# Side steps of one stage left to the products of the next, in a decoder block on one NeuronCore

## The chip, the cores and the metric

The kernel runs on one core of one Trainium2 chip. The metric is the device time of one execution in microseconds (us). Beside it stands one execution taken by the hardware profiler, whose span goes from the first to the last instruction of the program. The engines are PE (TensorE, matrix products), DVE (VectorE), ACT (ScalarE), POOL (GpSimd) and SP (which issues most DMA transfers). PSUM is the memory into which PE writes its sums; the kernel uses it as two pools of four tiles of 128 x 512 floats.

## The reference

One decoder layer on 256 tokens with 2048 features, all in f32:

```python
proj = rmsnorm(h, g_mix) @ w_in              # q, k, v, z, xBC, dt, two gates
out_a = attention(q, k, v) @ w_attn_br       # sliding window, with sinks
out_s = rmsnorm(ssd(...) * silu(z), g_ssd) @ w_ssd_br
merged = sigmoid(g_a) * out_a + sigmoid(g_s) * out_s
h = h + merged @ w_o
f = rmsnorm(h, g_ffn)
h = h + (silu(f @ w_gate) * (f @ w_up)) @ w_down
gate = sigmoid(rmsnorm(h, g_ple) @ w_ple_gate)
h = h + gate * (p @ w_ple_proj)
out = rmsnorm(h, g_final)
```

## The kernel before

**Products.** Every f32 product is made of three: a number is split into a high part (fp32r) and the low rest, and hi x hi, hi x lo and lo x hi are summed. Activations lie transposed, features on partitions, in tiles of four k-blocks of 128 features (`uT`, `yT`, `mergedT`, `hT`, `actT`, `h2T`); weights come in pieces of 128 x 1024 (`wr`, loaded by SP, four buffers), are split by ACT (`wh`, four buffers) and DVE (`wl`, three buffers), and are used by twelve matmuls of 512 columns.

**Wide blocks.** From the gate projection on, the work is a row of `wide_block` calls (L280): 256 tokens x 1024 columns, which give four sums `c11, c12, c21, c22`. The loop runs over pairs of k-blocks, `kp` = 0 to 7 (0 to 5 in the last third of `w_down`). A plain pair takes two weight pieces and 24 matmuls. One or two pairs of each block, named by the argument `forms`, are done with fewer matmuls, 21, in the manner of Strassen and Winograd: they need four combined "token forms" of the activations (`token_forms`, L267) and four combined weights (`tr`, four DVE additions, then split into `th` and `tl`). These form pairs sum into four further PSUM tiles, `shared`; after the block's last form pair their contents are combined into `mid` (one ACT, four DVE instructions), and when the block is done, `settle` or `add_settled` (L358, L363) joins each of the four sums with its part of `mid` on DVE.

**Pools.** The first line of `wide_block` is `psum.reverse()`: the four sums of a block come from the pool that held the `shared` tiles of the block before, and its `shared` tiles and all `aux_tile()` calls come from the pool that held the settled sums of the block before.

**Side steps.** Small pieces of work are queued in `side` and taken out by `pump`, one after each twelve matmuls, or two after a form pair (L97). A step of `queue_flip` (L980) or of `hidden` (L1041) is one `transpose_pair` (L144): four PE transposes of 128 x 128 into an `aux_tile()`, the split on ACT and DVE, and for a form pair `token_forms`. `square_sum` (L1020) is a step of ACT work for a norm; `rsqrt_mean` is one small DVE and one POOL instruction that give its factors (`r2`, `r3`, `r4`). `drain()` runs all steps that are left at once; it stands outside the blocks, so that their `aux_tile()` calls come before the next `psum.reverse()`.

**Order of the stages.** Gate projection `GSO` (2 blocks, forms `UPAIRS`), `w_ssd_br` (2 blocks, forms `YPAIRS`), `w_o` (2 blocks, forms at `mforms`), then three thirds of the feed-forward part: 4, 4 and 3 calls of `hidden` (one block each, forms at `hforms`, pairs 2 and 5), and after each third two blocks of `w_down` (forms at `aforms`), then projections with `nblock`, a plain loop with the same pieces and pumps, for `w_ple_proj` and `w_ple_gate`. The steps that a stage's last block queues are drained at L1011 (`merged` to `mergedT`), L1036 (`h` to `hT`, two `square_sum`), after the `hidden` calls of each third (`act` to `actT`) and at L1081 (`h` to `h2T`, two `square_sum`): six places. Between two blocks of one stage, `hidden` to `hidden` or the first block of `w_o` to the second, the steps are pumped within the next block.

The order in which each engine gets its instructions is drawn up when the program is built, by a planner that goes by priority (the order in the text) and by what it expects to be ready; what it finds not ready it lets others pass.

Of the kernel before, what the change touches and what calls it, by code (L numbers as in the profile page):

```python
# [23 lines left out]
NB = 512  # L24
# [6 lines left out]
FFN = 5632  # L31
# [30 lines left out]
def block_kernel(ctx: ExitStack, tc: tile.TileContext, x, x_t, p_t, positions, vecs, rows, g_final,  # L62
# [14 lines left out]
    def big(shape, dtype=F32, name="big"):  # L77
        return big_p.tile(shape, dtype, name=name, tag="big")

    def roll(name="roll"):  # L80
        return roll_p.tile([P, NB], F32, name=name, tag="roll")
# [13 lines left out]
    side, heads = deque(), deque()  # L95
# [7 lines left out]
    def drain(*queues):  # L103
        for q in queues or (side,):
            while q:
                q.popleft()()
# [22 lines left out]
    def split_to(dst, j0, ps, gains=None):  # L129

        if gains is None:
            nc.scalar.copy(out=dst[:, 0, j0:j0 + 2, :], in_=ps)
            nc.vector.tensor_tensor(out=dst[:, 1, j0:j0 + 2, :], in0=ps,
                                    in1=dst[:, 0, j0:j0 + 2, :].bitcast(F32), op=ALU.subtract)
        else:
            for j in range(2):
                nc.scalar.activation(out=dst[:, 0, j0 + j, :], in_=ps[:, j, :], func=AF.Copy,
                                     scale=gains[j])
                nc.vector.scalar_tensor_tensor(out=dst[:, 1, j0 + j, :], in0=ps[:, j, :],  # L139
                                               scalar=gains[j],  # L140
                                               in1=dst[:, 0, j0 + j, :].bitcast(F32),
                                               op0=ALU.mult, op1=ALU.subtract)
# [16 lines left out]
    def stat(tiles, k):  # L159
        return tiles[k // 4][:, 0, k % 4, :], tiles[k // 4][:, 1, k % 4, :]  # L160

    def mean_parts(n, eps, name):

        m = const.tile([P, NT, n + 1], F32, name=name)
        nc.vector.memset(m[:, :, n:n + 1], eps)
        return m
# [4 lines left out]
    def rsqrt_mean(parts, out_r):  # L171

        n = out_r.shape[1]
        s = stat_p.tile([P, NT], F32, name="rms_s")[:, :n]
        nc.vector.tensor_reduce(out=s, in_=parts, op=ALU.add, axis=AX.X)
        nc.gpsimd.tensor_tensor(out=out_r, in0=s, in1=mhalf[:, :n], op=ALU.pow)
# [82 lines left out]
    def joined(tiles, kp):  # L259

        ks = slice(2 * (kp % 2), 2 * (kp % 2) + 2)
        sc = roll("fsc").rearrange("p (j t) -> p j t", j=2)
        src = tiles[kp // 2].bitcast(F32)
        nc.vector.tensor_tensor(out=sc, in0=src[:, 0, ks], in1=src[:, 1, ks], op=ALU.add)
        return sc

    def token_forms(sc, dst):  # L267


        fm = roll("fm").rearrange("p (f t) -> p f t", f=4)  # L270
        a11, a21, a12, a22 = sc[:, 0, :P], sc[:, 0, P:], sc[:, 1, :P], sc[:, 1, P:]
        for o, x, y, op in ((fm[:, 0], a22, a21, ALU.subtract), (fm[:, 1], fm[:, 0], a11, ALU.add),
                            (fm[:, 2], a12, fm[:, 1], ALU.subtract),
                            (fm[:, 3], a11, a21, ALU.subtract)):
            nc.vector.tensor_tensor(out=o, in0=x, in1=y, op=op)
        nc.scalar.copy(out=dst[:, :, 0], in_=fm)
        nc.vector.tensor_tensor(out=dst[:, :, 1], in0=fm, in1=dst[:, :, 0].bitcast(F32),
                                op=ALU.subtract)
# [89 lines left out]
    def form_tiles(pairs, name):  # L368
        tile = big([P, 2, 4, 2, P], F32R, name=name)
        return {kp: tile[:, i] for i, kp in enumerate(pairs)}  # L370

    def column_pair(w, col0, jj):
        return tuple((w, col0 + (2 * jj + q) * NB) for q in range(2))
# [275 lines left out]
    ssq2 = mean_parts(GROUPS, SSM_EPS, "ssq2")  # L649
    GW = HPG * HD  # L650

    YPAIRS, yforms = (4,), {}

    def hslice(g):
        return slice(g * HPG, (g + 1) * HPG)
# [299 lines left out]
            nc.scalar.activation(out=merged[t][:, cols(j)], in_=accs[0][t], func=AF.Sigmoid,  # L955
                                 scale=r1[:, t:t + 1])
    drain(heads)
    UPAIRS = (2, 5)
    uforms = {}

    def u_forms(kp):
        def run():
            if kp == UPAIRS[0]:
                uforms.update(form_tiles(UPAIRS, "uforms"))
            token_forms(joined(uT, kp), uforms[kp])
        return run

    side.extend(u_forms(kp) for kp in UPAIRS)
    r2 = const.tile([P, NT], F32, name="r2")
# [10 lines left out]
    def queue_flip(src, dst, j, gbase=None, forms={}):  # L980
        for i in range(2):
            def run(i=i):
                if i == 0:
                    dst.extend(feat_tiles(1, "flipT"))
                gains = None
                if gbase is not None:
                    gains = [vcol(gbase, 4 * j + 2 * i + jj) for jj in range(2)]
                transpose_pair(src, j * NB + i * 2 * P, dst[j], 2 * i, gains, forms.get(2 * j + i))
            side.append(run)

    gates = []
    for jj in range(2):
# [3 lines left out]
            nc.scalar.activation(out=parts[i], in_=parts[i], func=AF.Sigmoid,  # L996
                                 scale=r1[:, i // 2:i // 2 + 1])
        gates.append(parts)
    mforms = form_tiles((4,), "mforms")
    for jj in range(2):  # L1000
        sums, parts = wide_block(column_pair(w_ssd_br, 0, jj), lambda k: stat(yT, k), KD, yforms)
        for i in range(4):
# [5 lines left out]
                                    op=ALU.add)  # L1008
        for q in range(2):
            queue_flip(merged, mergedT, 2 * jj + q, None, mforms)  # L1010
    drain()  # L1011


    h = [big([P, D], F32, name="h") for _ in range(NT)]
# [5 lines left out]
    def square_sum(j, ssq):  # L1020
        for t in range(NT):
            junk = roll("junk")
            nc.scalar.activation(out=junk, in_=h[t][:, cols(j)], func=AF.Square, scale=D ** -0.5,
                                 accum_out=ssq[:, t, j:j + 1])

    def add_to_h(jj, sums, parts):
        for i in range(4):
            add_settled(i, h[i // 2][:, cols(2 * jj + i % 2)], sums, parts)

    ssq3 = mean_parts(4, EPS, "ssq3")  # L1030
    for jj in range(2):
        add_to_h(jj, *wide_block(column_pair(w_o, 0, jj), lambda k: stat(mergedT, k), KD, mforms))
        for q in range(2):
            queue_flip(h, hT, 2 * jj + q, V_GFFN, hforms)
            side.append(lambda j=2 * jj + q: square_sum(j, ssq3))
    drain()  # L1036
    r3 = const.tile([P, NT], F32, name="r3")
    rsqrt_mean(ssq3, r3)


    def hidden(j, dst, kp0, forms):  # L1041
        sums, parts = wide_block(((w_gate, j * NB), (w_up, j * NB)), lambda k: stat(hT, k), KD,
                                 hforms)
        act = [roll("act") for _ in range(NT)]
        for i in range(4):
            settle(i, sums, parts, None if i % 2 else act[i // 2])
        for t in range(NT):
            nc.scalar.activation(out=act[t], in_=act[t], func=AF.Silu, scale=r3[:, t:t + 1])
            nc.vector.scalar_tensor_tensor(out=act[t], in0=parts[2 * t + 1],
                                           scalar=r3[:, t:t + 1], in1=act[t], op0=ALU.mult,  # L1050
                                           op1=ALU.mult)
        for i in range(2):
            side.append(lambda i=i: transpose_pair(act, i * 2 * P, dst, 2 * i, None,
                                                   forms.get(kp0 + i)))

    ssq4 = mean_parts(4, EPS, "ssq4")
    h2T, pT, gfin = [], None, None
    thirds = ((0, 4, (2, 5)), (4, 8, (2, 5)), (8, FFN // NB, (3,)))
    for j0, j1, apairs in thirds:
        last = j1 == FFN // NB  # L1060
        actT = []
        aforms = form_tiles(apairs, "aforms")
        for j in range(j0, j1):
            actT.append(big([P, 2, 4, SEQ], F32R, name="actT"))
            hidden(j, actT[-1], 2 * (j - j0), aforms)
        drain()
        if last:
            pT = [big([P, 2, 2, SEQ], F32R, name="pT")]
            pt = roll("pt").rearrange("p (j t) -> p j t", j=2)
            nc.gpsimd.dma_start(out=pt, in_=p_t)  # L1070
            split_to(pT[0], 0, pt)
            gfin = big([P, D], F32, name="gfin")
            nc.gpsimd.dma_start(out=gfin, in_=g_final.partition_broadcast(P))
        for jj in range(2):
            add_to_h(jj, *wide_block(column_pair(w_down[j0 * NB:j1 * NB], 0, jj),
                                     lambda k, a=actT: stat(a, k), 4 * (j1 - j0), aforms))
            if last:
                for q in range(2):
                    queue_flip(h, h2T, 2 * jj + q, V_GPLE)
                    side.append(lambda j=2 * jj + q: square_sum(j, ssq4))  # L1080
    drain()  # L1081

    psum.reverse()
    r4 = const.tile([P, NT], F32, name="r4")
    rsqrt_mean(ssq4, r4)


    ssq5 = mean_parts(5, EPS, "ssq5")
# [167 lines left out]
```

## Time and profile before

| | us |
|---|---|
| median of 3 runs | 1613.75 (1613.52 to 1614.44) |
| the profiled execution, its own time | 1613.52 |
| its span, first to last instruction | 1611.8 |
| PE busy | 1578.9 (98%) |
| DVE busy | 1202.3 (75%) |
| ACT busy | 845.7 (52%) |
| POOL busy | 130.3 (8%) |
| mean granted TensorE clock | 0.994 |

The matmuls' ends are modelled, so that PE's busy share says little by itself; starts that follow one another at an even distance say that PE is kept fed. The time of the execution is 1.7 us over its span.

### The profile page before, as it was taken

How to read it: one execution, taken by the hardware profiler on the slowest of the kernel's cores; microseconds unless marked ns; L12 is line 12 of the kernel's file. 1: busy time of each engine (PE TensorE's matmuls, PEld its weight loads, DVE VectorE, ACT ScalarE, POOL GpSimd, SP SyncE). 2: the span in 40 equal slices, each digit the busy share in tenths (PEclk: the TensorE clock that was granted, in tenths of full speed). 3: DMA queues.
4: the chain of work that ended last, by engine and by line, in shares of the span. 5: the costliest groups of instructions: out<-in, count | busy, mean ns of one | idle time of the engine just before them, and what ended most of it. 6: DMA issues, size and time to landing. Idle time of an engine off the chain costs nothing.

```text
span 1611.8 us, 19994 instructions
## 1 busy us (share of the span) xinstructions
PE 1578.9 (98%) x7294; PEld 1305.7 (81%) x7294; DVE 1202.3 (75%) x1507; ACT 845.7 (52%) x1073; POOL 130.3 (8%) x136
## 2 busy tenths in 40 slices
PE   9999999999999999999999999999999999999997
PEld 7988888888888788788788878788887888878786
DVE  8676776666766777777878888777888787878664
ACT  6654666455643554445555554445554445545553
POOL 1015233144110000000000000000000000000000
PEclk9999999999999999999999999999999999999999
DMA  8666435555556665555566655666665566655563
GB/s 271 174 194 183 143 105 157 157 169 154 163 173 180 208 197 195 208 188 190 161 199 188 198 180 187 201 202 196 196 196 182 189 197 202 210 180 193 180 210 106
DMA packets 152562, 296.63 MB, mean 184 GB/s; under 512 B 9536, under 2 KB 9664, under 8 KB 152080
## 3 DMA queue, kind: packets, MB, share of 16 engines
q1 hardware_dynamic: 151168, 290.76, 58.0%
q0 software_dynamic: 576, 3.47, 0.6%
q8 instruction: 57, 0.93, 0.2%
q10 hardware_dynamic: 720, 1.14, 0.2%
q14 instruction: 41, 0.34, 0.1%
HBM read 293.23 MB, written 2.10 MB: 183 GB/s over the span
## 4 chain that ended last, share of the span: by engine, by line
PE 94%; DVE 2%; ACT 2%; DMA 1%; issue 1%; POOL 0%; POOLq 0%; DVEq 0%; ACTq 0%
PE aux L248 30%; PE acc L248 28%; PE acc L204 9%; PE acc L205 9%; PE acc L206 9%; PE aux L150 1%; DMA wr<-in_w_ple_gate_dram 1%; PE aux L739 1%; PE aux L920 1%; PE acc L233 1%; PE acc L235 0%; PE acc L234 0%; PE aux L233 0%; PE aux L678 0%; PE aux L234 0%
## 5 line engine op out<-in xcount | busy, mean ns | idle before, releaser
L308 ACT CAST wh<-wr 128x1024 fp32r<-128x1024 f32 x280 | 294.0, 1054 | 285.2 <-PE aux L248 109.4
L310 DVE TENSOR_TENSOR wl<-wr,wh 128x1024 fp32r<-128x1024 f32 x280 | 338.8, 1221 | 83.2 <-PE aux L248 27.7
L195 DVE TENSOR_TENSOR wl<-wr,wh 128x1024 fp32r<-128x1024 f32 (+1 forms) x172 | 227.3, 1328 | 126.8 <-PE acc L205 96.9
L193 ACT CAST wh<-wr 128x1024 fp32r<-128x1024 f32 (+1 forms) x172 | 173.8, 1014 | 175.0 <-PE acc L206 136.6
L248 PE MATMUL aux<-wh,flipT 128*128 128x512 f32 x736 | 238.0, 394 | 2.5 <-DVE flipT L139 1.5
L248 PE MATMUL acc<-wh,flipT 128*128 128x512 f32 x640 | 208.3, 392 | 0.0
L204 PE MATMUL acc<-wh,uT 128*128 128x512 f32 (+1 forms) x512 | 200.2, 391 | 0.7 <-ACT cb L466 0.7
L206 PE MATMUL acc<-wh,uT 128*128 128x512 f32 (+1 forms) x512 | 194.0, 379 | 0.0
L205 PE MATMUL acc<-wl,uT 128*128 128x512 f32 (+1 forms) x512 | 193.8, 379 | 0.0
L248 PEld LDWEIGHTS aux<-wh,flipT 128*128 128x128 f32 x736 | 139.3, 189 | 32.3 <-issue 2.0
L248 PE MATMUL aux<-wl,flipT 128*128 128x512 f32 x368 | 144.3, 392 | 0.0
L248 PEld LDWEIGHTS acc<-wh,flipT 128*128 128x128 f32 x640 | 120.2, 188 | 24.5
L336 ACT CAST wh<-wr 128x1024 fp32r<-128x1024 f32 x80 | 66.9, 837 | 122.0 <-PE acc L248 62.3
L248 PE MATMUL acc<-wl,flipT 128*128 128x512 f32 x320 | 124.6, 389 | 0.0
L337 DVE TENSOR_TENSOR tl<-tr,th 128x2048 fp32r<-128x2048 f32 x40 | 91.7, 2291 | 26.9 <-ACT th L336 26.7
L204 PEld LDWEIGHTS acc<-wh,uT 128*128 128x128 f32 x512 | 96.3, 188 | 18.2 <-issue 1.4
L205 PEld LDWEIGHTS acc<-wl,uT 128*128 128x128 f32 x512 | 96.3, 188 | 17.6 <-issue 1.0
L206 PEld LDWEIGHTS acc<-wh,uT 128*128 128x128 f32 x512 | 96.2, 188 | 17.8
L336 ACT CAST th<-tr 128x2048 fp32r<-128x2048 f32 x40 | 76.5, 1913 | 54.9 <-DVE tr L328 54.9
L248 PE MATMUL aux<-wh,actT 128*128 128x512 f32 x292 | 94.4, 392 | 0.0
L248 PE MATMUL acc<-wh,actT 128*128 128x512 f32 x292 | 93.7, 392 | 0.0
L328 DVE TENSOR_TENSOR tr<-wr 128x512 f32<-128x512 f32 x80 | 52.5, 688 | 53.3 <-DMA wr<-in_w_down_dram 21.2
(471 smaller groups left out, 2765.3 us busy)
## 6 DMA issues: line engine op xcount, KB each, us to landing
wr<-in_w_in_dram SPq DMA_DIRECT2D x144, 512.0 KB, 3.7
wr<-in_w_gate_dram SPq DMA_DIRECT2D x88, 512.0 KB, 3.8
wr<-in_w_up_dram SPq DMA_DIRECT2D x88, 512.0 KB, 4.1
wr<-in_w_down_dram SPq DMA_DIRECT2D x88, 512.0 KB, 3.9
wr<-in_w_ssd_br_dram SPq DMA_DIRECT2D x32, 512.0 KB, 4.1
wr<-in_w_o_dram SPq DMA_DIRECT2D x32, 512.0 KB, 4.4
wr<-in_w_ple_gate_dram SPq DMA_DIRECT2D x32, 512.0 KB, 4.4
wr<-in_w_in_dram SPq DMA_DIRECT2D x32, 256.0 KB, 4.1
```

The lines of the kernel that those rows point to most:

```text
L150: nc.tensor.transpose(out=ps[:, j, t * P:(t + 1) * P], in_=src[t][:, c:c + P], identity=ident)
L193: nc.scalar.copy(out=wh, in_=wr)
L195: nc.vector.tensor_tensor(out=wl, in0=wr, in1=wh.bitcast(F32), op=ALU.subtract)
L204: nc.tensor.matmul(o, hi[:, ts], wh[:, kk, cs], start=(k == 0), stop=False)
L205: nc.tensor.matmul(o, hi[:, ts], wl[:, kk, cs], start=False, stop=False)
L206: nc.tensor.matmul(o, lo[:, ts], wh[:, kk, cs], start=False, stop=(k == nk - 1))
L248: nc.tensor.matmul(self.tile, a, b, start=self.first, stop=self.left == 0)
L308: nc.scalar.copy(out=wh, in_=wr)
L310: nc.vector.tensor_tensor(out=wl, in0=wr, in1=wh.bitcast(F32), op=ALU.subtract)
L328: nc.vector.tensor_tensor(out=o, in0=x, in1=y, op=ALU.add)
L336: nc.scalar.copy(out=xh, in_=x)
L337: nc.vector.tensor_tensor(out=xl, in0=x, in1=xh.bitcast(F32), op=ALU.subtract)
```

## The change

Six `drain()` calls are taken out. What was left in `side` is then pumped within the first pairs of the next stage's block, after its `psum.reverse()`. The two `rsqrt_mean` calls for `r3` and `r4` become side steps behind them. Form pairs are named one pair later: `YPAIRS`, `UPAIRS`, `mforms` and the `aforms` of all thirds; `hforms` stays.

```diff
-    YPAIRS, yforms = (4,), {}
+    YPAIRS, yforms = (5,), {}
...
-    UPAIRS = (2, 5)
+    UPAIRS = (3, 6)
...
-    mforms = form_tiles((4,), "mforms")
+    mforms = form_tiles((5,), "mforms")
...
         for q in range(2):
             queue_flip(merged, mergedT, 2 * jj + q, None, mforms)
-    drain()
...
             side.append(lambda j=2 * jj + q: square_sum(j, ssq3))
-    drain()
     r3 = const.tile([P, NT], F32, name="r3")
-    rsqrt_mean(ssq3, r3)
+    side.append(lambda: rsqrt_mean(ssq3, r3))
...
-    thirds = ((0, 4, (2, 5)), (4, 8, (2, 5)), (8, FFN // NB, (3,)))
+    thirds = ((0, 4, (3, 6)), (4, 8, (3, 6)), (8, FFN // NB, (4,)))
...
             hidden(j, actT[-1], 2 * (j - j0), aforms)
-        drain()
         if last:
             pT = [big([P, 2, 2, SEQ], F32R, name="pT")]
...
                     side.append(lambda j=2 * jj + q: square_sum(j, ssq4))
-    drain()
 
     psum.reverse()
     r4 = const.tile([P, NT], F32, name="r4")
-    rsqrt_mean(ssq4, r4)
+    side.append(lambda: rsqrt_mean(ssq4, r4))
```

## Rows read from the trace of the kernel before

**Rows 1.** The page: span, and the chain that ended last, by engine.

```profile
span 1611.8 us, 19994 instructions
...
PE 94%; DVE 2%; ACT 2%; DMA 1%; issue 1%; POOL 0%; POOLq 0%; DVEq 0%; ACTq 0%
```

**Rows 2.** PE's waits, whole span: who for whom, us in total, times, longest.

```profile
PE aux L150 <- DVE act L1049: 5.0, 2, 2.5
PE acc L150 <- DVE act L1049: 2.5, 1, 2.5
...
PE acc L248 <- DVE wl L337: 1.2, 1, 1.2
PE aux L248 <- DVE wl L337: 1.1, 1, 1.1
```

**Rows 3.** PE by stretch, the six drains: stretch, length, busy (count), granted clock, DMA.

```profile
672.82:684.35 11.53, 8.04 (x31) 0.70 0.23 74
769.23:779.18 9.95, 7.69 (x34) 0.83 0.35 104
947.54:957.07 9.53, 7.03 (x35) 1.00 0.38 124
1209.49:1219.02 9.53, 7.03 (x35) 1.00 0.38 124
1426.68:1440.10 13.42, 10.92 (x45) 0.87 0.38 119
1497.89:1508.04 10.15, 7.66 (x42) 1.00 0.36 125
```

**Rows 4.** PE by stretch: starts of the second blocks of w_ssd_br, w_o and hidden.

```profile
628.22:642.16 13.94, 13.94 (x70) 1.00 0.48 152
724.03:745.18 21.15, 21.15 (x102) 1.00 0.54 176
817.06:826.20 9.14, 9.14 (x45) 1.00 0.60 172
```

**Rows 5.** The chain there, hidden to hidden: start, us, what, count.

```profile
817.90 2.72 PE acc L248 x12
...
820.74 0.69 PE acc L248 x3
821.43 0.33 PE aux L150 x3
```

**Rows 6.** Timeline of PE at the first hidden-to-w_down drain: start, us, instruction, [idle before].

```profile
947.54 0.39 PE L248 MATMUL acc<-wh,flipT 128*128 128x512 f32 x1
950.43 0.44 PE L150 MATMUL aux<-ident,act 128*128 128x128 f32 x2 [2.50 <-DVE act L1049]
950.62 0.48 PE L248 MATMUL aux<-wh,actT 128*128 128x512 f32 x1
```

**Rows 7.** DVE by stretch: busy (count); form pair to block end, block start to form pair.

```profile
606.28:628.00 21.72, 14.96 (x17) 1.00 0.61 197
751.59:769.46 17.87, 14.79 (x18) 1.00 0.68 196
769.46:786.89 17.43, 14.68 (x26) 0.90 0.43 129
1037.39:1048.33 10.94, 8.94 (x11) 1.00 0.65 190
```

**Rows 8.** DVE groups from 495 to 1497: instruction, count | busy, mean ns | idle before.

```profile
L310 DVE TENSOR_TENSOR wl<-wr,wh 128x1024 fp32r<-128x1024 f32 x280 | 338.8, 1221 | 83.2 <-PE aux L248 27.7 <-issue 24.6 <-PE acc L248 20.8
L337 DVE TENSOR_TENSOR tl<-tr,th 128x2048 fp32r<-128x2048 f32 x40 | 91.7, 2291 | 26.9 <-ACT th L336 26.7
L337 DVE TENSOR_TENSOR wl<-wr,wh 128x1024 fp32r<-128x1024 f32 x80 | 76.3, 954 | 5.9 <-PE aux L248 3.3 <-PE acc L248 2.2
L328 DVE TENSOR_TENSOR tr<-wr 128x512 f32<-128x512 f32 x80 | 52.5, 688 | 53.3 <-DMA wr<-in_w_down_dram 21.2 <-DMA wr<-in_w_up_dram 17.4 <-DMA wr<-in_w_in_dram 10.7
```

**Rows 9.** DVE in the six stretches of rows 3, summed: length, busy, mean.

```profile
sum 64.11, DVE 50.87; mean DVE 8.48
```

## The prediction

> **What bounds the kernel now.** The page first: the chain that ended last is PE for 94% of the span [rows 1], so time is saved only where PE stands or runs slowly. PE's waits come next [rows 2]: the longest are on `act`, the last product of a `hidden` block's settling, 2.5 us each time. They stand where the text has a `drain()`. The third view puts a stretch around each of the six drains, from the start of the last product before the stop to the start of a product after it [rows 3]; the reader is to compare its length with the work in it. The fourth view does the same at starts of blocks where the steps left over are already pumped, not drained [rows 4, 5].
>
> A price for the work: twelve products take 2.72 us [rows 5], 0.2267 each. In the second block of `w_ssd_br` 13.94 us held 70 counted matmuls, of which one began earlier: four steps of 4 transposes, 16, and 53 products. 53 x 0.2267 = 12.01, so a transpose, change of kind included, is 1.93 / 16 = 0.12 us [rows 4]. With these prices the other two stretches come out without loss: 85 products and 16 transposes 21.19 of 21.15 us, 36 and 8 9.12 of 9.14 us [rows 4].
>
> **The change part by part.** *The six drains.* Each count of rows 3 holds one matmul that began earlier; of the rest 16 or 8 are transposes (four or two steps), the others products.
> - `w_ssd_br` to `w_o`: 14 products, 16 transposes, 5.09 us of work in 11.53: 6.44 lost.
> - `w_o` to `hidden`: 17 and 16, 5.77 in 9.95: 4.18 lost.
> - `hidden` to `w_down`, first and second third: 26 and 8, 6.85 in 9.53: 2.68 lost, twice.
> - the same in the last third: 36 and 8, 9.12 in 13.42: 4.30 lost.
> - `w_down` to `w_ple_proj`: 25 and 16, 7.59 in 10.15: 2.56 lost.
>
> Together 22.84 us. Three stretches have a mean granted clock of 0.70, 0.83 and 0.87, so part of each ran at the lower of the two levels (1.2 and 2.4 GHz) after PE had stood; the last third pays 4.30 where the same stop at full clock costs 2.68 [rows 3]. That part goes with the stop.
>
> Why PE stood: the drained steps wait for data that DVE is still settling, and the next block's four sums are to come from the pool that the steps use. At the first third PE stands 2.50 us, does two transposes, and then products that need nothing from them [rows 6]. After the change the sums come from the pool of the `shared` tiles, free since `mid`, and the steps use the settled sums' pool. The first twelve products start at once; a step's turn comes 2.72 us after the end of the last block, which was 947.54 + 0.23 = 947.77, thus at 950.49, where PE could begin transposing at 950.43 [rows 6]. So the step is covered, as between `hidden` blocks, where it lost nothing [rows 4, 5]. What is late next is DVE: its work in the six stretches, 50.87 of 64.11 us [rows 9], now lies beside products.
>
> *Moved with the drains:* 18 transposing steps with their splits and forms, four `square_sum`, two `rsqrt_mean`. Their PE work stays in the sum above. They issue no DMA; SP's queue holds weight loads in the same order, POOL gets two small instructions that no product waits for before the end of the next block. The split of `pT` now stands ahead of the last third's steps; it is counted in that boundary's residue.
>
> *Residue at the boundaries.* For `w_o` to `hidden`: the form pair at `kp` 2 needs `tl`. PE reaches it after 48 + 9 products and 16 transposes, 57 x 0.2267 + 1.92 = 14.84 us from the block's start; before, DVE needed 17.43 us with 14.68 busy [rows 7]. DVE fully packed is in time, as slow as before it is 2.59 late: 0 to 2.6, I take the middle, 1.3. In that block a new wait is possible too: the fourth step's tile may have to wait until a `shared` tile goes, after `kp` 5; its result is needed at `kp` 7, and `kp` 6 covers it with 24 products, 5.44 us. It is nothing, unless the splits queue behind more DVE work than that. For the five others 0, as rows 4 show, up to 1.0 each; I take 0.2 each, 1.0.
>
> *The form pairs one later:* 18 of the 40 pairs (GSO 4, `w_ssd_br` 2, `w_o` 2, `w_down` 10). A form pair is 21 products, 4.76 us on PE, and 4 x 0.688 + 2 x 0.954 + 2.29 = 6.95 us on DVE; a plain pair 5.44 and 2 x 1.22 = 2.44 [rows 8]. Between a form pair and the end of its block DVE had 6.8 and 3.1 us idle [rows 7]; one plain pair less there takes 5.44 - 2.44 = 3.0 of it. So DVE ends the block just about caught up, and the work for the next block's first pair starts no later, but for the two places where pair 6 of `w_down` is followed by pair 2 of `hidden`: there DVE had 2.0 us idle ahead of the pair [rows 7], and 3.0 goes: 0 to 1.0 each, I take 0.5, together 1.0. Two moved pairs wait now, 1.2 and 1.1 us, for a weight split [rows 2]; they may lose or keep that, and others may get it: from -2.3 (both gone) to +4.8 (four more), I take 0, since 16 of 18 show none.
>
> *Sum:* 22.84 - 1.3 - 1.0 - 1.0 = 19.5 us. The profiled execution took 1613.5 (span 1611.8 and 1.7 around it), 0.2 under the median: 1613.5 - 19.5 = 1594.0, on the median's scale 1594.2.
>
> **The rivals.**
> - *DVE is the bound at the boundaries.* If what DVE did while PE stood is paid by PE later, only DVE's own idle time is won: 64.11 - 50.87 = 13.2 us [rows 9], 1600.4. For it: DVE was busy 8.6 of 9.5 us there. Against it: rows 4, with DVE work of the same kind and no loss.
> - *Steps hold up the products behind them.* Between `hidden` blocks the first transpose ran at its turn and three products, 0.69 us, came before the next three [rows 5]. Were the order fixed, these would have waited. The Trainium skill, TensorE: Matmul & The Clock Gate, step-by-step list of Part 2, says that matmuls stay in program order and only weight loads are pulled ahead; that PE stood at transposes with free products behind them [rows 6] agrees. The planner put the three products there; should it expect the data too early at the new places, each of the six pays at least 0.69 us, 4.1 in all: 1598.3.
> - *The change does nothing.* The planner goes by readiness, so the same steps may be put first again: 1613.7. Against it: the sums no longer share a pool with the steps.
> - *Slower: a moved form pair meets the end of its block on DVE.* A pair takes DVE 6.95 us for PE's 4.76, 2.19 too much, worked off in plain pairs; now one fewer lies between it and the settling. If nothing is worked off, each of 18 pairs waits 2.19 us, 39.4 in all: 1594.2 + 39.4 - 2.3 = 1631. It turns the gain into a loss from 1.1 us a pair. Against it: the 3.1 to 6.8 us idle [rows 7].
>
> **How the numbers follow.** Forecast 0.72, DVE the bound 0.12, steps hold up 0.06, nothing 0.06, form pairs slower 0.04. The forecast's own bounds are 1613.7 - 22.8 - 2.3 = 1588.6 and 1594.2 + 1.3 + 4.0 + 1.0 + 4.8 = 1605.3; the first two rivals lie within. I give 1589 to 1604. A measurement of this kernel tells about 0.2%, 3.2 us, from no change: faster 0.90, same 0.06, slower 0.04.
>
> **What would show it.** Right: in stretches around the six places PE's starts follow evenly, twelve products, a step, twelve products; the waits on `act` L1049, `merged` and `flipT` are gone; granted clock 1.00 there, `act` steps 2.7 us after the block's end. Residue shows as PE waits on `tl` or `wl` L337 in the first form pair of the first `hidden` and of the two after `w_down`. Wrong: waits on `wl` L310 in the first pairs after a boundary (DVE the bound), on transposes (steps hold up), or on L337 in most moved pairs (slower).

## The result, and the profile after

The changed kernel takes 1596.29 us (median of four executions, 1594.48 to 1596.97) beside 1614.10 us for the kernel before: a ratio of 0.9887, with a 95% interval of 0.9870 to 0.9905. The profiled execution took 1596.97 us, with a span of 1595.3 us. Against the span of 1611.8 us [rows 1] that is 16.5 us less.

The page of the kernel after (span; busy time, share and instructions of an engine; shares of the chain that ended last):

```profile
span 1595.3 us, 19976 instructions
...
PE 1574.4 (99%) x7294; PEld 1300.2 (82%) x7294; DVE 1200.7 (75%) x1507; ACT 845.1 (53%) x1073; POOL 132.1 (8%) x136
...
PE 93%; DMA 2%; DVE 2%; ACT 2%; issue 1%; POOL 0%; POOLq 0%; DVEq 0%; ACTq 0%
```

DVE's busy time is the same as before within 2 us, and PE's share of the chain too: nothing was taken off an engine, a stop was.

PE by stretch, the kernel after, at the six places of [rows 3]. Each stretch runs from the last product of the old block to a product after the steps (in the second row after three of the four, since the fourth comes at 794.9 us); columns as there:

```profile
673.89:690.10 16.21, 16.21 (x80) 1.00 0.50 159
763.30:786.64 23.34, 22.80 (x105) 1.00 0.55 173
938.69:947.64 8.95, 8.95 (x45) 1.00 0.55 180
1199.09:1208.04 8.95, 8.95 (x45) 1.00 0.56 184
1416.83:1426.01 9.18, 9.18 (x46) 1.00 0.57 185
1483.69:1502.09 18.40, 18.40 (x90) 1.00 0.56 180
```

In five of them PE is busy from end to end, at the full clock level. The third holds 45 matmuls of which one began earlier: 8 transposes and 36 products, 36 x 0.2267 + 8 x 0.12 = 9.12 us of work by the prediction's prices, in 8.95. (A stretch whose end falls on a change of kind is 0.1 to 0.2 off by these prices; by the starts of single instructions 0.02 to 0.03 us is lost in each of the five.) Only `w_o` to `hidden`, the second row, still loses 1.2 us. So the six places lost 22.84 us before and about 1.3 after.

What happens in that second row is not what its small loss suggests. PE, then DVE, in the first `hidden` block (start, us, instruction, [idle before]):

```profile
784.17 0.85 PE L248 MATMUL acc<-th,hforms 128*128 128x512 f32 x3
786.28 0.39 PE L248 MATMUL acc<-tl,hforms 128*128 128x512 f32 x1
```

```profile
783.66 2.29 DVE L337 TENSOR_TENSOR tl<-tr,th 128x2048 fp32r<-128x2048 f32 x1 [0.58 <-ACT th L336]
```

The block's first product starts at 763.47. At 777.81, 14.3 us later, PE has done the two plain pairs, three steps and the first nine products of the form pair at `kp` 2, and the products with `th` and `tl` would be next. But `tl` is ready at 785.95, 8.1 us later. PE does not stand for it: the planner has put the products of a plain pair in between, from 777.81 to 784.17, and what PE loses there is mostly a wait of 0.5 us for that pair's own split (`wl` L310, in the list of waits below).

The chain of the kernel after at the first `hidden`-to-`w_down` boundary (start, us, what, count), to be held against the stop in [rows 6]:

```profile
935.90 3.17 PE acc L248 x14
939.08 2.72 PE aux L248 x12
941.80 0.11 PE acc L150
941.91 0.69 PE aux L248 x3
942.61 0.33 PE acc L150 x3
```

The old block's sums were in `acc`. The new block's twelve products go into `aux`, at once, and the transposes into `acc`, 2.72 us later, when their data is there. It is the picture of [rows 5] with the pools' names exchanged.

PE's waits in the wide blocks, whole span (who for whom, us in total, times, longest):

```profile
PE acc L248 <- DVE wl L337: 3.6, 3, 1.5
...
PE aux L248 <- DVE tl L337: 0.8, 2, 0.5
...
PE aux L248 <- DVE wl L337: 0.6, 1, 0.6
PE aux L248 <- DVE wl L310: 0.5, 1, 0.5
```

The three waits on `act` L1049 of [rows 2], 7.5 us, are gone. The waits on `wl` L337, the weight split of a form pair, were 2.3 us in two places and are 4.2 in four. Summed over the starts in all 40 form pairs, what PE loses there went from 5.0 to 8.9 us (without 0.8 in the first `hidden` block, which is counted at its boundary). The 18 pairs that were moved lose 3.2 us more than before, the other 22 lose 0.7 more. That gives the account between the two profiles: 22.84 - 1.3 = 21.5 us won at the boundaries, 3.9 lost in form pairs, 0.6 lost before the first wide block, and 0.5 that lies in no one place: 16.5.

The largest new wait, in `w_ssd`'s second block. DVE, PE and ACT (start, us, instruction, [idle before]):

```profile
654.75 1.22 DVE L337 TENSOR_TENSOR wl<-wr,wh 128x1024 fp32r<-128x1024 f32 x1
656.81 2.29 DVE L337 TENSOR_TENSOR tl<-tr,th 128x2048 fp32r<-128x2048 f32 x1 [0.84 <-ACT th L336]
659.02 0.69 DVE L337 TENSOR_TENSOR wl<-wr,wh 128x512 fp32r<-128x512 f32 x1
```

```profile
657.86 0.39 PE L248 MATMUL acc<-wh,yforms 128*128 128x512 f32 x1
659.76 0.50 PE L248 MATMUL acc<-wl,yforms 128*128 128x512 f32 x1 [1.51 <-DVE wl L337]
```

```profile
654.87 1.91 ACT L336 CAST th<-tr 128x2048 fp32r<-128x2048 f32 x1 [5.24 <-DVE tr L328]
656.68 0.62 ACT L336 CAST wh<-wr 128x512 fp32r<-128x512 f32 x1
```

A form pair has three splits: 128x1024 (`raw[0]`), 128x512 (half of `raw[1]`) and 128x2048 (`th` and `tl`). ACT casts the high part of each, then DVE makes the low one. The small one, 0.69 us of work on DVE, is needed before `tl`, but it is done after it. Its cast was late already: ACT stood idle for 5.24 us, did `th`, and only then the small cast, which was still running when DVE began `tl`. The place behind `tl` alone does not make PE wait: the small split stands there in 14 of the 40 form pairs of the kernel after, and in 19 of the kernel before. The experiments ask what does.

### The profile page after: what moved, and what is told of

Its sections match the earlier page's. It is cut to its first block, busy times and chain, and to the rows that moved or that the text cites. A ratio compares the mean times of both kernels' runs of the same rounds, so it can differ in the third digit from the quotient of the medians.

```text
span 1595.3 us, 19976 instructions
## 1 busy us (share of the span) xinstructions
PE 1574.4 (99%) x7294; PEld 1300.2 (82%) x7294; DVE 1200.7 (75%) x1507; ACT 845.1 (53%) x1073; POOL 132.1 (8%) x136
## 4 chain that ended last, share of the span: by engine, by line
PE 93%; DMA 2%; DVE 2%; ACT 2%; issue 1%; POOL 0%; POOLq 0%; DVEq 0%; ACTq 0%
PE aux L248 30%; PE acc L248 27%; PE acc L204 9%; PE acc L205 9%; PE acc L206 9%; PE aux L150 1%; DMA wr<-in_w_down_dram 1%; DMA wr<-in_w_ple_gate_dram 1%; PE aux L739 1%; PE acc L150 1%; PE aux L920 1%; PE acc L233 0%; PE aux L233 0%; PE aux L234 0%; PE aux L235 0%
## 5 line engine op out<-in xcount | busy, mean ns | idle before, releaser
L310 DVE TENSOR_TENSOR wl<-wr,wh 128x1024 fp32r<-128x1024 f32 x280 | 337.1, 1220 | 86.7 <-issue 37.3
L337 DVE TENSOR_TENSOR tl<-tr,th 128x2048 fp32r<-128x2048 f32 x40 | 91.7, 2291 | 25.2 <-ACT th L336 25.2
L206 PEld LDWEIGHTS acc<-wh,uT 128*128 128x128 f32 x512 | 96.1, 188 | 17.8
```

The lines of the kernel that those rows point to most:

```text
L206: nc.tensor.matmul(o, lo[:, ts], wh[:, kk, cs], start=False, stop=(k == nk - 1))
L310: nc.vector.tensor_tensor(out=wl, in0=wr, in1=wh.bitcast(F32), op=ALU.subtract)
L337: nc.vector.tensor_tensor(out=xl, in0=x, in1=xh.bitcast(F32), op=ALU.subtract)
```

## The experiments

Ratios are to the kernel before, run on the same chip (1615 to 1616 us there).

**1 and 2. The two halves alone.** First the drains out, with the form pairs at their old places:

```diff
-    YPAIRS, yforms = (5,), {}
+    YPAIRS, yforms = (4,), {}
-    UPAIRS = (3, 6)
+    UPAIRS = (2, 5)
-    mforms = form_tiles((5,), "mforms")
+    mforms = form_tiles((4,), "mforms")
-    thirds = ((0, 4, (3, 6)), (4, 8, (3, 6)), (8, FFN // NB, (4,)))
+    thirds = ((0, 4, (2, 5)), (4, 8, (2, 5)), (8, FFN // NB, (3,)))
```

> The six drains are gone, the form pairs stay where they were (YPAIRS 4, UPAIRS 2 and 5, mforms 4, aforms 2 and 5, and 3). Theory: the whole gain is the drains', and the pairs named one later cost some of it (in the changed kernel eight form pairs wait 7.0 us in all, before it two waited about 3): 1592 to 1594, 2 to 4 us under the changed kernel, with no wait left at the six places. Rival: the pairs had to be moved because a pair at kp 2 right behind a boundary meets the steps' DVE work: then PE waits on tl or wl there, about 2 us at each of the places where a pair follows at kp 2, and the time is 1598 to 1602.

Then the other half: the kernel after with the drains and the two direct `rsqrt_mean` calls of before, and the pairs one later.

> The drains stay, only the form pairs are named one later. Theory: the pairs' own cost shows alone, 2 to 5 us over the kernel before: 1616 to 1619, in waits on wl and tl L337. Rival: a later pair costs nothing by itself, its waits in the changed kernel come from DVE work that the missing drains left: 1613 to 1615.

Drains alone: 1593.78 us, 0.9861 (0.9842 to 0.9880). Pairs alone: 1618.03 us, 1.0018 (1.0007 to 1.0029). So the drains bring all of the gain, and moving the pairs takes 2.8 us from it by the second run (1.1 to 4.7), 4.2 by the first against the change (0.9861 and 0.9887, with intervals that overlap), 3.2 by what the moved pairs lose in the two profiles. PE's waits with the pairs alone, where the drains' stop and the pairs' wait stand together:

```profile
PE aux L150 <- DVE act L1049: 5.0, 2, 2.5
PE acc L248 <- DVE wl L337: 4.6, 3, 2.0
```

With the drains alone the longest wait is on `tl`, and two places make up nearly all of what form pairs lose by waiting (2.1 us and 0.7 by the starts, in the pairs at `kp` 4 of `w_ssd`'s second block and of `w_o`'s first):

```profile
PE aux L248 <- DVE tl L337: 2.1, 2, 1.8
```

So with the drains gone a pair at its old place can wait too.

**3. Is it the pool?** The kernel before, every drain kept, but run in the other pool at the six places:

```diff
+    def drain_other():
+        psum.reverse()
+        drain()
+        psum.reverse()
...
-    drain()
+    drain_other()
```

> The kernel before with its six drains in place, but run with the two PSUM pools exchanged, so that the drained transposes write the pool of the settled sums and the next block's sums find theirs free. Theory: the shared pool kept the products back, so the order in the text matters little: 1594 to 1598, with products ahead of the first transposes at the six places. Rival: what helps is the later place in the text, and drained steps still go first whatever their pool: 1612 to 1615.

1590.43 us, 0.9847 (0.9829 to 0.9866): as much as taking the drains out, though the steps still stand ahead of the next block in the text. PE at the first `hidden`-to-`w_down` boundary of this kernel (its lines are 5 further down):

```profile
939.67 0.39 PE L253 MATMUL aux<-wh,actT 128*128 128x512 f32 x1
939.90 0.38 PE L155 MATMUL acc<-ident,act 128*128 128x128 f32 x2
940.03 0.47 PE L253 MATMUL aux<-wh,actT 128*128 128x512 f32 x1
```

Eleven products of the new block had started before the first transposes. The planner let them pass as soon as their four sums had another pool than the steps. Where the steps stand in the text is not what cost the time; the shared pool is. The time is even 4 to 8 us below what I had written; it keeps the pairs at their old places, so the 3 to 4 us of the first two runs are saved. Experiment 1 keeps them too and took 3.4 us more, with intervals that overlap; form pairs lose 3.0 us less here than there by the profiles.

**4. A place of its own for the small split.** The change, with the 128x512 split in two tiles of another pool, in place of half a `wh` and half a `wl` tile:

```diff
-                    (raw[1][:, 1:2], whi_p.tile([P, 2, NB], F32R, name="wh", tag="wh")[:, 1:2],
-                     wlo_p.tile([P, 2, NB], F32R, name="wl", tag="wl")[:, 1:2]),
+                    (raw[1][:, 1:2], roll_p.tile([P, 1, NB], F32R, name="oh", tag="roll"),
+                     roll_p.tile([P, 1, NB], F32R, name="ol", tag="roll")),
```

> The changed kernel, with the split of the single half weight of a form pair (128 x 512) in two tiles of the roll pool, not in a slot of the four wh and the three wl. Theory: the form pairs wait because this small split gets its slot only after tl is done, so that DVE does it 2.3 us late; with tiles of its own it comes ahead of tl, and of the 7.0 us of waits in form pairs some 5 go: 1590 to 1592. Rival: DVE is behind there in any case, and the order of tl and the small split only shifts the wait from one to the other: 1595 to 1598.

1586.97 us, 0.9823 (0.9806 to 0.9840), the fastest kernel of the study: 10 us below the change (6 to 14 by the two intervals), and 3 below the lower end of what I expected. All waits on L337 are gone from the list of PE's waits, and of the 10.1 us between the two profiles 7.2 lie in form pairs (9.7 lost in all 40 before, 2.5 now); no experiment places the rest. What changed can be read at ACT's part of the splits, from 495 to 1497 us (instruction, count | busy, mean ns | idle before, and who ended it). The kernel after, then this one:

```profile
L336 ACT CAST wh<-wr 128x1024 fp32r<-128x1024 f32 x40 | 42.2, 1054 | 90.8 <-PE aux L248 42.6 <-PE acc L248 34.7 <-DMA wr<-in_w_down_dram 11.6
L336 ACT CAST wh<-wr 128x512 fp32r<-128x512 f32 x40 | 24.8, 620 | 49.9 <-PE aux L248 21.4 <-PE acc L248 20.6 <-DVE wl L337 5.9
```

```profile
L336 ACT CAST wh<-wr 128x1024 fp32r<-128x1024 f32 x40 | 42.2, 1054 | 25.6 <-PE aux L248 11.4 <-PE acc L248 7.3 <-DVE ol L337 4.1
L336 ACT CAST oh<-wr 128x512 fp32r<-128x512 f32 x40 | 24.9, 623 | 58.3 <-DMA wr<-in_w_up_dram 27.5 <-DMA wr<-in_w_down_dram 18.2 <-DMA wr<-in_w_in_dram 6.9
```

In the change both casts sit idle until PE is done with something, that is, until a `wh` tile comes free: 77 of 91 us and 42 of 50. With tiles of its own, the small cast waits mainly for its data (DMA), and the other's wait for PE falls to 19 us. The work is the same to 0.1 us.

The same two rows of the kernel before:

```profile
L336 ACT CAST wh<-wr 128x1024 fp32r<-128x1024 f32 x40 | 42.2, 1055 | 83.6 <-PE acc L248 37.9 <-PE aux L248 37.4 <-issue 3.2
L336 ACT CAST wh<-wr 128x512 fp32r<-128x512 f32 x40 | 24.8, 620 | 38.4 <-PE acc L248 24.4 <-PE aux L248 13.5 <-ACT fsc L255 0.4
```

There the casts waited for PE nearly as long, 75 and 38 us. These rows show who waits for a tile, then, and not what the wait costs PE.

**5 and 11. Both together, and which pair.** The other pool of experiment 3 with the tiles of experiment 4:

> The kernel before with the drains in place but in the exchanged pools, the form pairs where they were, and the small split of a form pair in tiles of the roll pool. Theory: the two causes are separate and add: the exchange of the pools was worth 24 us of 1615, the small split's slot is behind what form pairs still wait (about 2 us there): 1586 to 1588, as the changed kernel with own tiles (1587), since neither has a wait left to lose. Rival: drained steps first in the text bring the weights of the first pairs late once no form wait hides it: 1590 to 1593.

1589.73 us, 0.9844 (0.9829 to 0.9859). That is no gain over experiment 3 that can be told, and not what I expected: the tiles, worth 10 us in the change, bring nothing here that can be measured. PE's waits are in two places, the `kp` 4 pairs of `w_ssd`'s second block and `w_o`'s first, on `tl`:

```profile
PE aux L253 <- DVE tl L342: 1.0, 1, 1.0
PE acc L253 <- DVE tl L342: 1.0, 1, 1.0
```

If these two pairs are too early, moving them alone should help:

```diff
-    YPAIRS, yforms = (4,), {}
+    YPAIRS, yforms = (5,), {}
-    mforms = form_tiles((4,), "mforms")
+    mforms = form_tiles((5,), "mforms")
```

> Pools exchanged at the drains and own tiles (e5, 0.9844 of before), and the form pairs of w_ssd_br and w_o at 5 in place of 4; those of the gate projection and w_down stay at 2 and 5, and 3. Theory: of e5's waits the two at pair 4, 2.3 us, come from a pair that stands too close behind a boundary with four steps; at 5 they go: 0.9825 to 0.9832. Rival: pair 5 brings DVE's work closer to the block's end and the wait comes back at the next boundary: 0.984 to 0.985.

1587.81 us, 0.9826 (0.9813 to 0.9839); the two waits are 0.2 us each. The intervals of the two runs overlap, but the place that I named changed. So with the small split in tiles of its own a later pair is not dearer in these two stages, while in the shared slots the later pairs cost 3 to 4 us (experiments 1 and 2). That speaks for the slots as a part of what the move costs. It is not a proof: only 4 of the 18 pairs are moved here, and the fuller test, experiment 4 with all 18 pairs at their old places, was not run.

**6. The tiles without the drains.** The kernel before with the edit of experiment 4.

> The kernel before, with only the small split of a form pair in tiles of the roll pool; drains, pools and pairs as before. Theory: two form pairs wait there, about 2.8 us in all, and these waits go: 0.9980 to 0.9985 of the kernel before. Rival: the drains' idle time already hides most DVE work and the small waits come back at the drains: 0.9995 to 1.0005.

1613.04 us, 0.9991 (0.9981 to 1.0000). It lies between what the theory and the rival say, and settles nothing between them. In its profile the two waits on `wl` L337 are gone, as the theory has it, a new one of 1.0 us is on `tl`, and form pairs lose 3.6 us in place of 5.0. The time says that before, with drains, the small split's place was worth 0 to 3 us, and after, without them and with the pairs later, 10.

**7 and 8. Single boundaries.** The change with one drain put back, `w_ssd` to `w_o`:

> The changed kernel with one drain put back, that between w_ssd_br and w_o. The first term of the sum alone: it lost 6.4 us with its slow clock; put back it costs 5.5 to 7 over the changed kernel (0.9887 of before): 0.992 to 0.993 of before. Rival: boundaries are not independent, DVE work put off at one is caught up at the next, so that one drain gives back only its idle time, 3.5 us or less: 0.990 to 0.991.

And with the three drains behind `hidden` put back:

> The changed kernel with the drains between hidden and w_down put back, in all three thirds. Three terms of the sum: 2.7, 2.7 and 4.3 us, 9.7 together, or 8.0 where the clock does not fall: 0.9937 to 0.9948 of before. Rival: the stop gives DVE time in which it gets ahead for w_down's form pairs, so that some 3 us of waits in them go and the drains cost 5 to 6.5: 0.9918 to 0.9928.

1602.34 us, 0.9920 (0.9905 to 0.9934), 5.3 us over the change; and 1607.45 us, 0.9947 (0.9933 to 0.9961), 9.7 us over it. The sum of the prediction has 6.44 for the first and 2.68 + 2.68 + 4.30 = 9.66 for the three. Each difference is good to about 4 us, so the terms hold in size, not to the tenth, and the time alone would also allow the first rival's 3.5 us. The trace of the seventh kernel decides (PE by stretch, columns as in [rows 3]):

```profile
672.01:683.36 11.35, 8.55 (x32) 0.70 0.22 78
```

That is 15 products and 16 transposes, 5.32 us of work by the prediction's prices, in 11.35: 6.0 lost, for 6.44 in the kernel before. The stop is back with its old length in the eighth kernel (its lines there are those of the kernel after, 2 above those of before):

```profile
PE aux L150 <- DVE act L1047: 5.0, 2, 2.5
PE acc L150 <- DVE act L1047: 2.5, 1, 2.5
```

**9 and 10. Is DVE the bound?** Experiment 4 with the DVE part of the split done several times in the 18 steps that the change moves (work done over again, to no effect), twice and four times (first part; the branch with gains is changed in the same way):

```diff
-            nc.vector.tensor_tensor(out=dst[:, 1, j0:j0 + 2, :], in0=ps,
-                                    in1=dst[:, 0, j0:j0 + 2, :].bitcast(F32), op=ALU.subtract)
+            for _ in range(times):
+                nc.vector.tensor_tensor(out=dst[:, 1, j0:j0 + 2, :], in0=ps,
+                                        in1=dst[:, 0, j0:j0 + 2, :].bitcast(F32),
+                                        op=ALU.subtract)
...
```

> The changed kernel with own tiles (e4, 0.9823 of before), in which each of the 18 steps that the change moves does its DVE split twice: 10 times 0.69 and 8 times two of 0.48, 14.6 us more DVE work, all right behind the six boundaries. Theory: DVE has idle time enough there and the products' lookahead covers it: 0.982 to 0.985. Rival (DVE is the bound at the boundaries): the work is paid in full, 0.9905 to 0.992.

> The same with the split four times, 43.7 us more DVE work behind the six boundaries, up to 11.5 at one with four steps. Theory: here the cover ends; at the boundaries with four steps DVE falls some 5 to 8 us behind and the form pairs that follow wait, at those with two steps little is lost: 12 to 24 us in all, 0.990 to 0.997. Rival (DVE is the bound from the start): 43.7 us in full, 1.009.

Twice: 1591.51 us, 0.9847 (0.9834 to 0.9860), 3.9 us more than experiment 4. Four times: 1601.35 us, 0.9905 (0.9892 to 0.9918), 13 us more. DVE's busy time rose by 11.8 and 34.8 us, less than the 14.6 and 43.7 that I had reckoned. If DVE had been the bound there, all of it would have been paid; about a third is (each difference is good to 3 to 4 us). Some 8 of the 13 us stand in one place, the first `hidden` block, where the DVE work of four steps meets a form pair at `kp` 2. Some of it is lost while the granted clock was at its lower level (0.50 from 781.62 to 788.45 us), and 5.3 us in these waits:

```profile
PE aux L252 <- ACT oh L340: 2.3, 1, 2.3
...
PE aux L252 <- DVE ol L341: 1.7, 1, 1.7
...
PE aux L252 <- ACT wh L312: 1.3, 1, 1.3
```

**12. Order or slots?** In experiment 4 the small split is also done earlier on DVE. So the change once more, with nothing but the order of the three splits turned, the small one first, still in `wh` and `wl` tiles:

```diff
-                    (raw[0], whi_p.tile([P, 2, NB], F32R, name="wh", tag="wh"),
-                     wlo_p.tile([P, 2, NB], F32R, name="wl", tag="wl")),
                     (raw[1][:, 1:2], whi_p.tile([P, 2, NB], F32R, name="wh", tag="wh")[:, 1:2],
                      wlo_p.tile([P, 2, NB], F32R, name="wl", tag="wl")[:, 1:2]),
+                    (raw[0], whi_p.tile([P, 2, NB], F32R, name="wh", tag="wh"),
+                     wlo_p.tile([P, 2, NB], F32R, name="wl", tag="wl")),
...
-            b11, b21, b22, t1, t3, t2, t4 = split
+            b22, b11, b21, t1, t3, t2, t4 = split
```

> The changed kernel, with the small split of a form pair still in a slot of wh and wl, but written first of the pair's three splits, so that DVE does it ahead of tl in every pair. Theory: the order costs the waits, so most of what own tiles brought comes without them: 0.983 to 0.985 of before (the changed kernel 0.9887, own tiles 0.9823). Rival: own tiles helped because they leave one more slot of wh and wl to the plain pairs' weights; then the order alone gives little: 0.987 to 0.989.

1600.67 us, 0.9905 (0.9889 to 0.9922): no better than the change, whose interval it overlaps, and nearer to the rival's range, which ends at 0.989, than to the theory's 0.983 to 0.985. My theory that the order is the cause falls. DVE at the same form pair of this kernel:

```profile
658.19 0.68 DVE L337 TENSOR_TENSOR wl<-wr,wh 128x512 fp32r<-128x512 f32 x1
660.25 2.29 DVE L337 TENSOR_TENSOR tl<-tr,th 128x2048 fp32r<-128x2048 f32 x1 [1.38 <-ACT th L336]
662.46 1.22 DVE L337 TENSOR_TENSOR wl<-wr,wh 128x1024 fp32r<-128x1024 f32 x1
```

Now the large split comes behind `tl`, and PE wants it sooner than the small one:

```profile
PE aux L248 <- DVE wl L337: 3.7, 2, 2.0
PE acc L248 <- DVE wl L337: 2.8, 4, 1.4
```

And DVE's group for the large split, from 495 to 1497 us (columns as in [rows 8]), says what it had waited for:

```profile
L337 DVE TENSOR_TENSOR wl<-wr,wh 128x1024 fp32r<-128x1024 f32 x40 | 48.9, 1223 | 17.8 <-PE acc L248 9.5 <-PE aux L248 8.2
```

These 17.8 us, ended by PE, were 2.0 in the kernel after, 1.1 of them ended by PE. At this pair the one that is second in the text ends up behind `tl`, as in the kernel after; over all 40 pairs that is so for the large one in 7 here, for the small one in 14 there. Both use whole tiles of the same two pools (four `wh`, three `wl`), and the second gets its tiles only when PE has let earlier ones go; meanwhile `th` and `tl`, which have tiles elsewhere, can pass it. By this reading, what experiment 4 took away is that second claim. That a fifth `wh` or a fourth `wl` tile would do the same wasn't tried.

## Why the prediction was right, point by point

- *The drains, 22.84 us.* Right: about 21.5 came, by the stretches. The single places, put back, cost 5.3 by the times and 6.0 by the stretch, for 6.44, and 9.7 by the times for 9.66 (experiments 7 and 8).
- *Why PE stood: one pool for the steps and the next sums.* Shown: with the pool exchanged and the drains kept, the gain is there (experiment 3). "The change does nothing" falls with it.
- *The order at the boundary,* twelve products and then a step 2.72 us behind the block's end: as forecast at the `hidden`-to-`w_down` boundary, to the count, with three products between the first transpose and the next three.
- *Residue at `w_o` to `hidden`,* 1.3 forecast, 1.2 measured: the number is right by luck. PE reached the form pair when the prediction said, but `tl` came 8.1 us after its turn, not 0 to 2.6; DVE took 22.5 us from the block's start, 17.7 of them busy, where the prediction reckoned with 14.68 to 17.43. What kept the loss small is a plain pair that the planner put in between, which the prediction did not have.
- *Residue elsewhere.* The other five boundaries 1.0 forecast, 0.1 measured; the pairs of `hidden` behind `w_down` 1.0 forecast, 0.9 measured from the block's start to the end of the pair, 0.4 of it in the pairs themselves. The fourth step of the first `hidden` block did wait for a `shared` tile: its transposes stand at 794.9 us, in the middle of the form pair at `kp` 5, just after the first `shared` tile had been read. It cost nothing, as said.
- *DVE the bound.* Falls: in the changed kernel five boundaries lose nothing, and in experiments 9 and 10 about a third of added DVE work is paid. The sign that was named for it, a wait on `wl` L310 behind a boundary, did show once, with 0.5 us, at `w_o` to `hidden`, where the cover is thinnest.
- *Steps hold up the products.* Not seen. The planner again let products pass.
- *The moved form pairs, 0 (from -2.3 to +4.8).* This is the term that was mis-sized. It is +3.2 by the profiles and +2.8 by experiment 2, inside the bounds, towards their upper end. What failed in the step is what was counted, DVE's amount of work and its idle time up to the end of the block; the tiles that the splits fill were left out. In the changed kernel, tiles of its own for the small split take away most of what form pairs lose (experiment 4: 9.7 us to 2.5), and doing it first on DVE does not (experiment 12). Why a pair one later loses more by it is not shown. Neither the idle time of ACT's casts, nearly the same in the kernel before, nor the number of small splits behind `tl`, which went down, tells the two kernels apart.

Between the two profiles 16.5 us were won, 3.0 less than the 19.5 of the sum: 1.0 more at the boundaries (1.3 left for 2.3 forecast), 2.9 less in form pairs (3.9 lost in all, for the 1.0 that stood for those behind `w_down`), 0.6 ahead of the wide blocks and 0.5 that no row accounts for. On the medians the miss is 2.1 us, since the profiled execution of before lies 0.2 under the median that the forecast went by, and that of after 0.7 over its own.

## What to carry to other kernels

Work left over at a stage's end should get its PSUM tiles from another pool than the next stage's first sums: then it can be late without holding the products up; here that held whether it stood ahead of the next stage in the program or within it. Before a piece of work is moved because an engine has time for it, look at the buffers that it fills as well: a small tile that takes a full-size slot can make other tiles late. Idle time of the engine that fills the slot, ended by the engine that empties it, says where to look, not what it costs. Giving such a tile a place of its own was worth 10 us in the changed kernel, more than half of what the change brought, but 0 to 3 us in the kernel before and nothing measurable beside the exchanged pools: what one wait is worth depends on which others are left.

## What the runs showed of the hardware that I had not expected

The same stop does not always cost the same clock. Three times a kernel with drains stops 2.50 us for `act`; PE in the 8 us behind each stop, first the kernel before, then the one of experiment 2 (stretch, length, busy (count), granted clock, DMA):

```profile
950.43:958.43 8.00, 8.00 (x39) 1.00 0.38 128
1212.38:1220.38 8.00, 8.00 (x39) 1.00 0.38 125
1429.57:1437.57 8.00, 8.00 (x32) 0.79 0.22 67
```

```profile
947.55:955.55 8.00, 8.00 (x32) 0.79 0.20 71
1215.02:1223.02 8.00, 8.00 (x33) 0.80 0.22 74
1435.72:1443.72 8.00, 8.00 (x32) 0.79 0.22 73
```

Behind one of the three the granted clock went to its lower level for a part of the 8 us in the one profile, behind all three in the other, in experiment 8 behind the first alone, and in experiment 6 behind the first and the third: 7 of 12. Where it did, 32 or 33 matmuls were begun in place of 39: about 7 x 0.2267 = 1.6 us. So the 4.30 us that the prediction has for the last third, 1.62 more than for the others, belong to that execution and not to that place; a sum over several stops of this kind carries 1.6 us of doubt for each. A shorter stop was followed by it as well: in experiment 1 PE waited 1.82 us for `tl` in a form pair, and from 657.70 to 661.11 us the granted clock was 0.50, while behind the 1.51 us of the kernel after (659.76 us) it stayed at 1.00.
